# Gated-output copies kept in their traced order, and a new slot order in the recurrence, of a two-layer hybrid trunk

## The chip, the cores and the metric

The kernel runs on one core of one Trainium2 chip. The metric is the device time of one execution in microseconds (us); lower is better. The core's engines run side by side, each through its own queue in order: TensorE (PE) does the matrix products, VectorE (DVE), ScalarE (ACT) and GpSimd (POOL) the element-wise work, and SyncE (SP) starts the transfers (DMA).

## The reference

One sequence of 1024 positions and 1024 features in float32 goes through two layers and a last norm. Each layer is `x = x + gate(c) * mixer(rmsnorm(x) * (1 + scale(c)) + shift(c))`, where shift, scale and gate are products of `silu(c)` with a matrix. Layer 0 is attention: eight heads of windowed attention (A) and eight of forgetting attention (B, softmax with a decay), whose outputs are gated and go through one output projection:

```
y = jnp.concatenate([a_out, b_out], axis=-1) * jax.nn.silu(gate)
return y @ w_out
```

Layer 1 is a gated linear recurrence over positions. Its input product has 8 blocks of 128 features for the recurrence (`xr`) and 8 for the gate:

```
xc = conv_b
for j in range(CONV_WIDTH):
    xc = xc + xp[:, j:j + S] * conv_w[j]
r = sigmoid(xc_block @ w_a + b_a);  i = sigmoid(xc_block @ w_x + b_x)
log_a = -LRU_C * r * softplus(-lam);  a = exp(log_a)
u = sqrt(-expm1(2.0 * log_a)) * (i * xc)
hs[t] = a[t] * hs[t - 1] + u[t]
y = (hs * silu(gate)) @ w_out
```

## The kernel before

**Products.** Every float32 operand is written as a sum of a high and a low part in the format that PE multiplies at full rate. Of a weight, ACT copies the high part (`whi_...`) and POOL subtracts it from the raw one, which leaves the low part (`wlo_...`). Each block of 128 x 128 weights then takes three matmuls: high x high, low x high, high x low. Activations are split in the same way (`yh`/`yl`, `y1h`/`y1l`, `xch`/`xcl`, `pth`/`ptl`). A "copy" below is ACT's making of a high part, a "subtraction" that of a low one.

**Layer 0.** The attention heads are written out as a list of small steps, and `weave` mixes into them the matmuls of the next projection (`fill`), so that PE has work while softmax goes on. In the stretch that matters here (the seventh call of `weave`, 420 to 460 us) PE runs the last B heads: scores `sB`, transposes of the probabilities `ptB`, which `split_t` splits into `pth_B` and `ptl_B`, and the product with the values, `oB`. Mixed in are the last weights of K and V (`khb`, `klb`, `vb`) and the output projection of the first half of the positions (`ps_fill<-yh,...`, weights `whi_o0a`, `wlo_o0a`). That projection needs the gated outputs `gy` of finished heads in split form: `split_act` copies `yh` on ACT and subtracts `yl` on POOL. Six such splits are put in a list `drip`, and `fill` takes one off it every eighth matmul. Their place on an engine is not the place in the code: here a scheduler orders the instructions of ACT, by its own simulated times, except those that are issued under `paced("act")`.

**Layer 1.** From `ordered |= ALL` on, every engine keeps the order of the code. `slot(c)` does feature block c: sigmoids `r`, `i` and `th` on ACT, `a`, `a2`, the square root, `hs` by a scan on DVE; meanwhile PE makes the input products of block c+2 (`ps_lx`, with the convolution's taps on DVE into `xc`) and the gate product of block c (`ps_lg`, in two halves h of 512 positions). The gated output of one half is made in three steps: `gate_s` (sigmoid `sg` on ACT, a multiplication by `ps_lg` on DVE), `gate_a` (times `hs`, on POOL), `gate_b` (copy `y1h` on ACT, subtraction `y1l` on POOL). `split_next` splits the next 128 columns of weights in two halves (`whi_lg` twice on ACT, `wlo_lg` twice on POOL, or `lx`); `split_r` splits the small weights of r and i (`wrh`, `wrl`). `mod_late` is a dot product of the late rows of the modulation on DVE. `last_slot(7)` has no `ps_lx`; it splits the first weights of the output product, `whi_wo`/`wlo_wo` by `split_next` and the later ones by `split_out(e)`. Then the output product of the first half of the positions (`ps_o`) runs over e = 0 to 7 with k over the 8 feature blocks. For e below `AHEAD` its last feature block, k = 7, is put off until the first seven blocks of all these e are through.

In the text, t0(c) is the start of DVE's multiplication `sg_r<-ps_lg,sg_r` of half 0 in slot c; the loop's period is the distance from one to the next.

Of the kernel before, what the change touches and what calls it, by code (L numbers as in the profile page):

```python
# [3 lines left out]

# [1 line left out]

# [13 lines left out]
EARLY = 12  # L20
NS = 5
FIRST = 18
AHEAD = 3
RUN = 32
P = 128
S = 1024
# [22 lines left out]
def hybrid_trunk(  # L49
# [53 lines left out]
    def copy(out, in_, scale=1.0):  # L103
        act.activation(out, in_, AF.Copy, scale=scale)
# [612 lines left out]
    def scores(ps, q, n, kh, kl, ks):  # L717
# [2 lines left out]
        mm(ps, q[:, nq], kh[:, ks], start=True, stop=False)  # L720
        mm(ps, q[:, nq], kl[:, ks], start=False, stop=True)

    def split_t(pt, w, name):
        hi = at.tile([P, HALF], F32R, tag="pth", name=f"pth_{name}")
        lo = at.tile([P, HALF], F32R, tag="ptl", name=f"ptl_{name}")
        copy(hi[:, :w], pt[:, :w])
        sub(dve, lo[:, :w], pt[:, :w], r32(hi[:, :w]))
        return hi, lo

# [217 lines left out]
    def fill(jobs, ahead=lambda: None):  # L947

        jobs = list(jobs)
        ws = {0: jobs[0][0]()}  # L950
        for n, (_, ks, xs, use) in enumerate(jobs):
            if n + 1 < len(jobs):
                ws[n + 1] = jobs[n + 1][0]()
            else:
                ahead()
            w = ws.pop(n)
            for h, (xhi, xlo) in xs().items():
                ps = ps_mm(f"ps_fill_{h}")
                cnt = 0
                for k in ks:  # L960
                    whi, wlo = w[k]
                    for i, (a, b) in enumerate(((whi, xhi), (wlo, xhi), (whi, xlo))):
                        mm(ps, a, b[:, k], start=(k == ks[0] and i == 0), stop=(k == ks[-1] and i == 2))
                        cnt += 1
                        if late and cnt == 9:
                            late.pop()()
                        if drip and cnt % 8 == 0:
                            drip.popleft()()
                        yield MM
                x = use(h, ps)  # L970
                if x:
                    late.append(x)
# [120 lines left out]
    def total(js):  # L1093
        return sum(len(ks) * 3 * len(list(xs())) * MM for _, ks, xs, _ in js)
# [262 lines left out]

    def mod_late(c):
        mod_row(late_rows.pop(c), 24 + c)
        load_row(c + 2)  # L1360

    def rt(tag, c, dt=F32, w=S, bufs=1):
        return rp.tile([P, w], dt, tag=tag, name=f"{tag}_r{c}", bufs=bufs)
# [66 lines left out]
    def gate_a(c, h, eng=gp):  # L1430

        mul(eng, sgs[c, h], sgs[c, h], hss[c][:, half(h)])
# [9 lines left out]
        load_next()  # L1442
    load_r(0)
    load_row(0)
    load_row(1)
    for c in range(2):
        conv(c, 0, ps01[c])()
    split_xc(0, half(0))
# [15 lines left out]
    def slot(c):  # L1464
        n = c + 2
        w = ready.popleft()
        if c == 0:
            ps_x = proj1(0, f"lx_{n}", 0, w)
        ps = gates(c)
        if c == 0:  # L1470
            split_next()
        else:
            gate_s(c - 1, 1)
            gate_a(c - 1, 1)
        r, i_ = sig_ri(c, ps)

        th, a_, a2 = rt("th", c), rt("a", c), rt("a2", c)
        act.activation(th, r, AF.Tanh, scale=sp[:, c : c + 1])
        mul(dve, i_, i_, xcs[c])
        split_xc(c + 1)  # L1480
        split_r(c + 1)
        if n < KT:
            load_r(n)
        if c:
            gate_b(c - 1, 1)
        act.activation(a_, r, AF.Exp, scale=nsp[:, c : c + 1])
        if c:
            split_next()
        if n < KT:
            taps = conv(n, 0, proj1(0, f"lx_{n}", 0, w) if c else ps_x)  # L1490
        act.activation(a2, a_, AF.Square)
        if n < KT:
            taps()
        dve.scalar_tensor_tensor(out=th, in0=a2, scalar=1.0, in1=th, op0=ALU.add, op1=ALU.mult)
        act.activation(th, th, AF.Sqrt, bias=tiny)
        mul(dve, i_, i_, th)
        hs_ = hss[c] = rt("hs", c, bufs=2)
        dve.tensor_tensor_scan(out=hs_, data0=a_, data1=i_, initial=0.0, op0=ALU.mult, op1=ALU.add)
        if n < KT:
            conv(n, 1, proj1(0, f"lx_{n}", 1, w))()  # L1500
            w = ready.popleft()
            split_next()
        lgs[c, 0] = proj1(0, f"lg_{c}", 0, w)
        gate_s(c, 0)
        gate_a(c, 0)
        if n < KT:
            gate_b(c, 0)
        mod_late(c)
        lgs[c, 1] = proj1(0, f"lg_{c}", 1, w)

    def last_slot(c):

        w = ready.popleft()
        ps = gates(c)
        for h in range(2):
            lgs[c, h] = proj1(0, f"lg_{c}", h, w)
        r, i_ = sig_ri(c, ps)
        split_next()
        wout.append(ready.popleft())
        gate_s(c - 1, 1)  # L1520
        gate_b(c - 1, 0)
        th, a_, a2 = rt("th", c), rt("a", c), rt("a2", c)
        act.activation(th, r, AF.Tanh, scale=sp[:, c : c + 1])
        mul(dve, i_, i_, xcs[c])
        gate_s(c, 0)
        gate_a(c - 1, 1)
        act.activation(a_, r, AF.Exp, scale=nsp[:, c : c + 1])
        mod_late(c)
        act.activation(a2, a_, AF.Square)
        gate_b(c - 1, 1)  # L1530
        dve.scalar_tensor_tensor(out=th, in0=a2, scalar=1.0, in1=th, op0=ALU.add, op1=ALU.mult)
        split_out(1, dve)
        act.activation(th, th, AF.Sqrt, bias=tiny)
        mul(dve, i_, i_, th)
        hs_ = hss[c] = rt("hs", c, bufs=2)
        dve.tensor_tensor_scan(out=hs_, data0=a_, data1=i_, initial=0.0, op0=ALU.mult, op1=ALU.add)
        split_out(2)
        gate_a(c, 0, dve)
        gate_s(c, 1)
        gate_b(c, 0, dve)  # L1540
        gate_a(c, 1, dve)
        split_out(3)
        gate_b(c, 1, dve)

    for c in range(KT - 1):
# [6 lines left out]
    for t0, tw in ((0, 512), (512, 256), (768, 256)):  # L1552
# [7 lines left out]
        for e in range(KT):  # L1560
            if t0 == 0 and e + 4 < KT:
                split_out(e + 4)
            w = wout[e]
            nm = f"ps_o1_{t0}_{e}"
            ps = (ps_s, ps_t)[e % 2](nm) if t0 == 0 and e <= AHEAD else ps_1(nm)
            last = KT - 1 if t0 == 0 and e < AHEAD else KT
            gemm(ps[:, :tw], w, y1h[:, :, ts], y1l[:, :, ts], range(last), last=(last == KT))
            late_.append((e, w, ps))
            if t0 == 0 and e + 1 < AHEAD:
                continue  # L1570
            for e_, w_, ps in late_:
# [94 lines left out]
```

## Time and profile before

| | |
|---|---|
| median of 3 runs | 886.59 us (886.31 to 886.68) |
| the profiled execution | 888.44 us |
| its span, first to last instruction | 886.7 us |
| PE busy | 860.7 us, 97% of the span |
| DVE, ACT, POOL busy | 564.5, 535.7, 378.1 us (64%, 60%, 43%) |
| mean granted clock of PE | 0.986 |

Of PE's time 3% is waiting, but a matmul at the lower clock also counts as busy. So two things are read together: the idle time that stands in square brackets behind an instruction, with the engine and tile that ended it, and the granted clock of a stretch (PEclk; 1.00 is 2.4 GHz, 0.50 is 1.2 GHz). All instructions of this kernel carry line L85, so they are told apart by the names of their tiles; out stands left of the arrow, in right of it.

### The profile page before, as it was taken

Reading aid. Unit: us, or ns where it says so; the run is one execution under the profiler, and the core shown is the slowest. Engines: PE = TensorE matmul, PEld = TensorE weight load, DVE = VectorE, ACT = ScalarE, POOL = GpSimd, SP = SyncE. Lnnn points to the kernel's source line nnn. Section 1 sums busy time; section 2 is a strip of 40 time slices with the busy share of each in tenths; the row PEclk is TensorE's granted clock in tenths of the full one; section 3 lists DMA queues with packets and bytes.
Section 4 is the critical chain, followed back from the end, with each engine's and each line's share of the span. In section 5 each row is a group of like instructions: output and inputs, shape, how many; then the busy total and the mean of one; then the engine's idle time right before and its main releaser. Section 6 shows DMA issues by size and latency. Waiting matters only on the chain.

```text
span 886.7 us, 13483 instructions
## 1 busy us (share of the span) xinstructions
PE 860.7 (97%) x4618; PEld 730.7 (82%) x4618; DVE 564.5 (64%) x1136; ACT 535.7 (60%) x1047; POOL 378.1 (43%) x427
## 2 busy tenths in 40 slices
PE   9999999999989999999999999999899999999995
PEld 8887898888878888888777888878688877878995
DVE  7886657688676565565656668276556666583453
ACT  5765124788676666566656647358666667774432
POOL 4843322343342232331744656532565555475100
PEclk9999999999999999999999999999899999999998
DMA  9944772100013322322373564421212212126042
GB/s 344 404 185 127 216 229 60 49 25 20 30 53 111 107 80 101 123 87 78 110 240 104 184 209 145 145 79 44 78 54 72 77 57 67 56 71 226 7 149 83
DMA packets 54620, 103.83 MB, mean 117 GB/s; under 512 B 6960, under 2 KB 20720, under 8 KB 54040
## 3 DMA queue, kind: packets, MB, share of 16 engines
q1 hardware_dynamic: 53400, 101.93, 34.8%
q10 hardware_dynamic: 1152, 1.05, 0.5%
q8 instruction: 36, 0.59, 0.3%
q14 instruction: 32, 0.26, 0.1%
HBM read 94.02 MB, written 8.93 MB: 116 GB/s over the span
## 4 chain that ended last, share of the span: by engine, by line
PE 66%; ACT 11%; DVE 10%; DMA 5%; POOL 4%; issue 3%; SPq 0%; DVEq 0%; POOLq 0%; ACTq 0%
PE ps_fill L85 22%; PE ps_o L85 10%; PE pst L85 5%; PE ps_o0c L85 5%; PE oB L85 4%; PE sB L85 4%; PE ptB L85 3%; DVE xc_r L85 3%; PE ps_v L85 3%; DVE hs_r L85 2%; DMA ada<-in_ada_dram 2%; PE ps_lx L85 2%; POOL sg_r L85 2%; PE sA L85 2%; PE ps_lg L85 2%
## 5 line engine op out<-in xcount | busy, mean ns | idle before, releaser
L85 PE MATMUL ps_o<-y1h,wo 128*128 128x256 f32 (+1 forms) x336 | 76.8, 323 | 2.2 <-DVE wo L85 1.1
L85 DVE TENSOR_TENSOR ptl_B<-ptB,pth_B 128x512 fp32r<-128x512 f32 (+1 forms) x80 | 50.8, 636 | 36.8 <-ACT pth_B L85 36.3
L85 ACT ACTIVATE pth_B<-ptB 128x512 fp32r<-128x512 f32 (+1 forms) x80 | 44.0, 551 | 44.6 <-PE ptB L85 43.7
L85 ACT ACTIVATE pB<-pB,mnB 128x128 f32<-128x128 f32 (+3 forms) x64 | 49.5, 774 | 31.3 <-DVE mnB L85 25.9
L85 PEld LDWEIGHTS ps_o<-y1h,wo 128*128 128x128 f32 x336 | 56.7, 192 | 7.5 <-ACT wo L85 1.5
L85 POOL TENSOR_SCALAR_AFFINE_SELECT pB<-pB 128x128 f32<-128x128 f32 x64 | 18.8, 296 | 96.3 <-DMA pB<-gd 71.6
L85 PE MATMUL pst<-hh,ws 128*128 128x512 f32 x192 | 55.3, 396 | 0.1
L85 PE MATMUL ps_o<-y1l,wo 128*128 128x256 f32 (+1 forms) x168 | 54.2, 323 | 0.0
L85 PE MATMUL ps_lg<-h1h,wlo_lg 128*128 128x512 f32 x128 | 51.3, 401 | 2.3 <-POOL wlo_lg L85 2.3
L85 PE MATMUL ps_lg<-h1h,whi_lg 128*128 128x512 f32 x128 | 51.4, 401 | 1.9 <-ACT whi_lg L85 1.9
L85 DVE SCALAR_TENSOR_TENSOR xc_r<-ps_lx,col,xc_r 128x509 f32<-128x509 f32 (+2 forms) x48 | 35.7, 745 | 24.6 <-ACT xt_r L85 23.5
L85 PE MATMUL ps_lg<-h1l,whi_lg 128*128 128x512 f32 x128 | 50.8, 397 | 0.0
L85 PE MATMUL ps_lx<-h1l,whi_lx 128*128 128x512 f32 x128 | 50.3, 393 | 0.2 <-POOL h1l L85 0.2
L85 PE MATMUL ps_lx<-h1h,whi_lx 128*128 128x512 f32 x128 | 50.3, 393 | 0.0
L85 PE MATMUL ps_lx<-h1h,wlo_lx 128*128 128x512 f32 x128 | 50.1, 391 | 0.0
L85 DVE CUSTOM_DVE_ANT_0 pB<-sB,pB 128x384 f32<-128x384 f32 (+2 forms) x64 | 35.4, 554 | 19.4 <-PE sB L85 9.3
L85 ACT ACT_TABLE_LOAD x35 | 44.9, 1283 | 3.6 <-issue 1.9
L85 PE MATMUL ptB<-ident,pB 128*128 128x128 f32 x288 | 45.1, 273 | 1.2 <-DVE ptl_B L85 0.7
L85 PEld LDWEIGHTS ptB<-ident,pB 128*128 128x128 f32 x288 | 35.8, 140 | 12.2 <-PE rbT_B L85 1.5
L85 POOL TENSOR_TENSOR wlo_lx<-raw_lx,whi_lx 128x512 fp32r<-128x512 f32 x16 | 30.6, 1929 | 32.0 <-ACT whi_lx L85 30.1
L85 PEld LDWEIGHTS pst<-hh,ws 128*128 128x128 f32 x192 | 35.9, 188 | 9.0 <-DVE mod L85 0.6
L85 ACT ACTIVATE sq_o<-x 128x512 f32<-128x512 f32 (+1 forms) x33 | 18.0, 545 | 33.3 <-DVE x L85 33.1
(313 smaller groups left out, 2838.7 us busy)
## 6 DMA issues: line engine op xcount, KB each, us to landing
ada<-in_ada_dram SPq DMA_DIRECT2D x32, 512.0 KB
x<-in_xT_dram SPq DMA_DIRECT2D x20, 256.0 KB
ada<-in_ada_dram SPq DMA_DIRECT2D x4, 1024.0 KB
pB<-gd SPq DMA_DIRECT2D x8, 512.0 KB
raw_o0a<-in_wo_dram SPq DMA_DIRECT2D x16, 256.0 KB
raw_o0c<-in_wo_dram SPq DMA_DIRECT2D x16, 256.0 KB
x1d<-x SPq DMA_DIRECT2D x16, 256.0 KB
raw_lx<-in_wl_dram SPq DMA_DIRECT2D x16, 256.0 KB
```

The costliest lines, as they stand in the source:

```text
L85: ins = issue(*args, **kw)
```

## The change

1. A list `dripping` is filled during the last call of `weave`. While it is, the copies `pth` of `split_t` are issued under `paced("act")`, and so are the splits that `fill` takes off `drip`: these two kinds of copies keep their order of the code among each other on ACT.
2. In `slot(c)` the splits of the small weights and of the next gate weights come right behind the sigmoids r and i, and the gated output of slot c-1 is finished later: `gate_a` of half 1 and `gate_b` of both halves stand behind `split_xc` of slot c. Before, `gate_b` of half 0 was the end of slot c itself.
3. The late rows of the modulation are loaded one slot ahead, not two.
4. In `last_slot` the split of `wo_1` goes from DVE to POOL, `split_out(2)` and `(3)` come one step earlier, and the gated output of block 6 is finished later.
5. `AHEAD` is 4, not 3: k = 7 of e = 0, 1, 2 (9 matmuls) comes behind the k < 7 of e = 3 (21 matmuls).

The core of the diff:

```
     def split_t(pt, w, name):
...
-        copy(hi[:, :w], pt[:, :w])
+        with paced("act") if dripping else nullcontext():
+            copy(hi[:, :w], pt[:, :w])
...
                         if drip and cnt % 8 == 0:
-                            drip.popleft()()
+                            with paced("act"):
+                                drip.popleft()()
...
     for i in range(7):
+        dripping[:] = [1] * (i == 6)
         weave(slots[cuts[i] : cuts[i + 1]], fill(...), ...)
...
         ps = gates(c)
-        if c == 0:
-            split_next()
-        else:
+        if c:
             gate_s(c - 1, 1)
-            gate_a(c - 1, 1)
         r, i_ = sig_ri(c, ps)
+        split_r(c + 1)
+        if n < KT:
+            load_r(n)
+        split_next()
 
         th, a_, a2 = rt("th", c), rt("a", c), rt("a2", c)
         act.activation(th, r, AF.Tanh, scale=sp[:, c : c + 1])
         mul(dve, i_, i_, xcs[c])
         split_xc(c + 1)
-        split_r(c + 1)
-        if n < KT:
-            load_r(n)
         if c:
+            gate_a(c - 1, 1)
+            gate_b(c - 1, 0)
             gate_b(c - 1, 1)
         act.activation(a_, r, AF.Exp, scale=nsp[:, c : c + 1])
-        if c:
-            split_next()
...
         gate_a(c, 0)
-        if n < KT:
-            gate_b(c, 0)
         mod_late(c)
+        load_row(c + 1)
...
     def last_slot(c):
...
-        gate_a(c - 1, 1)
+        split_out(1)
...
-        gate_b(c - 1, 1)
...
-        split_out(1, dve)
+        split_out(2)
...
-        split_out(2)
+        gate_a(c - 1, 1)
+        split_out(3)
         gate_a(c, 0, dve)
         gate_s(c, 1)
         gate_b(c, 0, dve)
         gate_a(c, 1, dve)
-        split_out(3)
+        gate_b(c - 1, 1)
```

In layer 0, ACT's queue around the first splits of `gy` (in the last call of `weave`, near 420 us of the profile) read before:

```order
L85 ACTIVATE pth_B_3_2_4835<-ptB_3_2_4830 128x512
L85 ACTIVATE yh_4895<-gy_511 128x512 x4
L85 ACTIVATE khb_0_4855<-ps_fill_4728 64x512
L85 ACTIVATE yh_4895<-gy_511 128x512 x2
L85 ACTIVATE pth_B_3_3_4851<-ptB_3_3_4847 128x384
L85 ACTIVATE pth_B_0_0_4880<-ptB_0_0_4876 128x384
L85 ACTIVATE khb_0_4855<-ps_fill_4728 64x512
L85 ACTIVATE khb_1_4856<-ps_fill_4728 64x512
L85 ACTIVATE tmp<-oB_3_4823 64x256
```

and now:

```order
L85 ACTIVATE pth_B_3_2_4835<-ptB_3_2_4830 128x512
L85 ACTIVATE khb_0_4855<-ps_fill_4728 64x512
L85 ACTIVATE pth_B_3_3_4851<-ptB_3_3_4847 128x384
L85 ACTIVATE khb_0_4855<-ps_fill_4728 64x512
L85 ACTIVATE khb_1_4856<-ps_fill_4728 64x512
L85 ACTIVATE pth_B_0_0_4880<-ptB_0_0_4876 128x384
L85 ACTIVATE tmp<-oB_3_4823 64x256
L85 ACTIVATE yh_4895<-gy_511 128x512
L85 ACTIVATE tmp<-oB_0_4913 64x256
```

The six copies `yh` stood ahead of `pth_B_3_3` and `pth_B_0_0`; now none does, and the six come one by one behind later steps. Further on, `pth_B_1_1` now stands behind three `khb` copies and the two `whi_o0a` copies, where it stood ahead of them, and on DVE `ptl_B_3_1` of the following head stands ahead of the `pB_0` and `pB_1` that wait for a transfer.

In slot 1, ACT's queue from the second half of r on (c = 1; slots 2 to 5 have the same pattern) read before:

```order
L85 ACTIVATE r_r_7017<-psr_1_6998,col 128x512
L85 ACTIVATE i_r_7018<-psi_0_7005,col 128x512
L85 ACTIVATE i_r_7018<-psi_1_7006,col 128x512
L85 ACTIVATE th_r_7023<-r_r_7017,sp 128x1024
L85 ACTIVATE xch_r_7028<-xc_r_6881 128x1024
L85 ACTIVATE wrh_r_6874<-wr_r_6872 128x128
L85 ACTIVATE wrh_r_6878<-wr_r_6876 128x128
L85 ACTIVATE y1h<-sg_r_1_7013 128x512
L85 ACT_TABLE_LOAD
L85 ACTIVATE a_r_7024<-r_r_7017,nsp 128x1024
L85 ACTIVATE whi_lg_0_7047<-raw_lg_0_6851 128x512
L85 ACTIVATE whi_lg_1_7053<-raw_lg_1_6930 128x512
```

and now:

```order
L85 ACTIVATE r_r_7012<-psr_1_6994,col 128x512
L85 ACTIVATE i_r_7013<-psi_0_7001,col 128x512
L85 ACTIVATE i_r_7013<-psi_1_7002,col 128x512
L85 ACTIVATE wrh_r_6851<-wr_r_6849 128x128
L85 ACTIVATE wrh_r_6855<-wr_r_6853 128x128
L85 ACTIVATE whi_lg_0_7030<-raw_lg_0_6867 128x512
L85 ACTIVATE whi_lg_1_7036<-raw_lg_1_6928 128x512
L85 ACTIVATE th_r_7042<-r_r_7012,sp 128x1024
L85 ACTIVATE xch_r_7047<-xc_r_6879 128x1024
L85 ACTIVATE y1h<-sg_r_0_6961 128x512
L85 ACTIVATE y1h<-sg_r_1_7009 128x512
L85 ACT_TABLE_LOAD
```

The two `whi_lg` copies moved from behind `a` to ahead of `th`, and the two `y1h` copies stand together ahead of the table load.

On POOL, the same slot from the first gated half on read before (`sg_r_0`, `sg_r_1` are the halves' products with `hs`):

```order
L85 TENSOR_TENSOR sg_r_0_6963<-sg_r_0_6963,hs_r_6892 128x512
L85 TENSOR_TENSOR y1l<-sg_r_0_6963,y1h 128x512
L85 TENSOR_TENSOR sg_r_1_7013<-sg_r_1_7013,hs_r_6892 128x512
L85 TENSOR_TENSOR wrl_r_6875<-wr_r_6872,wrh_r_6874 128x128
L85 TENSOR_TENSOR wrl_r_6879<-wr_r_6876,wrh_r_6878 128x128
L85 TENSOR_TENSOR y1l<-sg_r_1_7013,y1h 128x512
L85 TENSOR_TENSOR wlo_lg_0_7048<-raw_lg_0_6851,whi_lg_0_7047 128x512
L85 TENSOR_TENSOR wlo_lg_1_7054<-raw_lg_1_6930,whi_lg_1_7053 128x512
L85 TENSOR_TENSOR wlo_lx_0_7130<-raw_lx_0_6936,whi_lx_0_7129 128x512
L85 TENSOR_TENSOR wlo_lx_1_7136<-raw_lx_1_7051,whi_lx_1_7135 128x512
```

and now:

```order
L85 TENSOR_TENSOR sg_r_0_6961<-sg_r_0_6961,hs_r_6890 128x512
L85 TENSOR_TENSOR wrl_r_6852<-wr_r_6849,wrh_r_6851 128x128
L85 TENSOR_TENSOR wrl_r_6856<-wr_r_6853,wrh_r_6855 128x128
L85 TENSOR_TENSOR wlo_lg_0_7031<-raw_lg_0_6867,whi_lg_0_7030 128x512
L85 TENSOR_TENSOR wlo_lg_1_7037<-raw_lg_1_6928,whi_lg_1_7036 128x512
L85 TENSOR_TENSOR sg_r_1_7009<-sg_r_1_7009,hs_r_6890 128x512
L85 TENSOR_TENSOR y1l<-sg_r_0_6961,y1h 128x512
L85 TENSOR_TENSOR y1l<-sg_r_1_7009,y1h 128x512
L85 TENSOR_TENSOR wlo_lx_0_7128<-raw_lx_0_6934,whi_lx_0_7127 128x512
L85 TENSOR_TENSOR wlo_lx_1_7134<-raw_lx_1_7034,whi_lx_1_7133 128x512
```

Both `y1l` and the product of half 1 moved behind the four weight splits; the two `wlo_lg` moved ahead of them.

## Rows read from the trace of the kernel before

**Rows 1.** The page, part 1: busy, share of the span, instructions.

```profile
PE 860.7 (97%) x4618; PEld 730.7 (82%) x4618; DVE 564.5 (64%) x1136; ACT 535.7 (60%) x1047; POOL 378.1 (43%) x427
```

**Rows 2.** One slot each: length, busy by engine, PEclk, DMA share, GB/s.

```profile
621.36:651.81 30.45, 27.97 (x109) 22.17 (x108) 20.37 (x27) 17.50 (x25) 16.91 (x12) 0.89 0.23 69
651.81:676.38 24.57, 24.57 (x109) 20.27 (x108) 14.47 (x18) 17.51 (x25) 14.37 (x10) 1.00 0.22 66
...
726.76:752.61 25.85, 25.00 (x109) 20.19 (x108) 15.75 (x19) 17.50 (x25) 14.89 (x10) 1.00 0.21 67
...
780.00:806.00 26.00, 23.82 (x97) 19.02 (x96) 18.03 (x16) 14.71 (x19) 17.23 (x11) 0.93 0.44 138
```

**Rows 3.** The same columns for three stretches behind a wait of PE.

```profile
424.13:429.00 4.87, 4.72 (x17) 4.09 (x18) 4.09 (x8) 2.48 (x6) 4.73 (x7) 0.65 0.39 118
...
637.00:644.20 7.20, 6.50 (x15) 4.81 (x16) 4.58 (x5) 5.92 (x10) 2.51 (x2) 0.53 0.25 74
...
786.00:791.00 5.00, 3.90 (x9) 2.87 (x10) 4.08 (x4) 3.42 (x4) 2.46 (x2) 0.66 0.31 103
```

**Rows 4.** PE, 424 to 456 us: start, took, instruction, [idle before].

```profile
424.13 0.44 PE L85 MATMUL oB<-pth_B,vb 128*128 128x256 f32 x2 [1.43 <-ACT pth_B L85]
...
450.10 0.41 PE L85 MATMUL rbT_B<-ident,rb_B 128*128 128x128 f32 x2 [0.86 <-DVE ptl_B L85]
...
455.09 0.50 PE L85 MATMUL oB<-ptl_B,vb 128*128 128x256 f32 x2 [1.15 <-DVE ptl_B L85]
```

**Rows 5.** ACT, order of time, 418 to 426 us.

```profile
422.56 1.13 ACT L85 ACTIVATE yh<-gy 128x512 fp32r<-128x512 f32 x2
423.61 0.84 ACT L85 ACTIVATE pth_B<-ptB 128x384 fp32r<-128x384 f32 x2
```

**Rows 6.** PE, order of time, 635 to 640 and 785 to 791 us.

```profile
637.11 0.75 PE L85 MATMUL ps_lg<-h1h,whi_lg 128*128 128x512 f32 x1 [1.89 <-ACT whi_lg L85]
638.45 0.80 PE L85 MATMUL ps_lg<-h1h,wlo_lg 128*128 128x512 f32 x1 [0.59 <-POOL wlo_lg L85]
...
786.00 0.49 PE L85 MATMUL ps_o<-y1h,wo 128*128 128x512 f32 x1 [1.08 <-ACT wo L85]
787.59 0.79 PE L85 MATMUL ps_o<-y1h,wo 128*128 128x512 f32 x1 [1.10 <-DVE wo L85]
```

**Rows 7.** DVE, order of time, 676 to 703 us (slot 3).

```profile
676.35 0.68 DVE L85 TENSOR_TENSOR sg_r<-ps_lg,sg_r 128x512 f32<-128x512 f32 x1
...
682.88 1.23 DVE L85 TENSOR_TENSOR i_r<-i_r,xc_r 128x1024 f32<-128x1024 f32 x1 [1.55 <-ACT i_r L85]
...
702.20 0.68 DVE L85 TENSOR_TENSOR sg_r<-ps_lg,sg_r 128x512 f32<-128x512 f32 x1
```

**Rows 8.** POOL, order of time, the same stretch.

```profile
677.12 2.27 POOL L85 TENSOR_TENSOR sg_r<-sg_r,hs_r 128x512 f32<-128x512 f32 x1 [2.52 <-DVE sg_r L85]
...
681.41 1.30 POOL L85 TENSOR_TENSOR sg_r<-sg_r,hs_r 128x512 f32<-128x512 f32 x1
685.11 1.72 POOL L85 TENSOR_TENSOR wrl_r<-wr_r,wrh_r 128x128 fp32r<-128x128 f32 x2 [2.40 <-ACT wrh_r L85]
...
688.81 2.55 POOL L85 TENSOR_TENSOR wlo_lg<-raw_lg,whi_lg 128x512 fp32r<-128x512 f32 x2 [0.71 <-ACT whi_lg L85]
695.91 4.52 POOL L85 TENSOR_TENSOR wlo_lx<-raw_lx,whi_lx 128x512 fp32r<-128x512 f32 x2 [4.55 <-ACT whi_lx L85]
```

**Rows 9.** ACT, order of time, the same stretch.

```profile
685.10 0.65 ACT L85 ACTIVATE y1h<-sg_r 128x512 fp32r<-128x512 f32 x1
...
688.12 1.13 ACT L85 ACTIVATE whi_lg<-raw_lg 128x512 fp32r<-128x512 f32 x2
```

**Rows 10.** ACT, order of time, 771 to 800 us.

```profile
774.93 1.27 ACT L85 ACTIVATE i_r<-psi,col 128x512 f32<-128x512 f32 x2 [0.67 <-DVE hs_r L85]
776.09 1.15 ACT L85 ACTIVATE whi_wo<-raw_wo 128x512 fp32r<-128x512 f32 x2
```

**Rows 11.** POOL, order of time, 771 to 800 us.

```profile
777.72 3.54 POOL L85 TENSOR_TENSOR wlo_wo<-raw_wo,whi_wo 128x512 fp32r<-128x512 f32 x2
```

More of the change, by code (lines that the diff above doesn't have):

```diff
@@ L2 @@
 import math
-from contextlib import ExitStack, contextmanager
+from contextlib import ExitStack, contextmanager, nullcontext
 import numpy as np
@@ L22 @@
 FIRST = 18
-AHEAD = 3
+AHEAD = 4
 RUN = 32
@@ L721, in scores @@
         mm(ps, q[:, nq], kl[:, ks], start=False, stop=True)
+    dripping = []
     def split_t(pt, w, name):
@@ L1174, in hybrid_trunk @@
     for i in range(7):
+        dripping[:] = [1] * (i == 6)
         weave(slots[cuts[i] : cuts[i + 1]], fill(jobs[i + 1], jobs[i + 2][0][0]), total(jobs[i + 1]), 0 if i else FIRST)
+    dripping.clear()
     def square_sum(sqa, xn, e, pool, name, tag="sq"):
@@ L1359, in mod_late @@
         mod_row(late_rows.pop(c), 24 + c)
-        load_row(c + 2)
     def rt(tag, c, dt=F32, w=S, bufs=1):
@@ L1444, in hybrid_trunk @@
     load_row(0)
-    load_row(1)
     for c in range(2):
@@ L1564, in hybrid_trunk @@
             nm = f"ps_o1_{t0}_{e}"
-            ps = (ps_s, ps_t)[e % 2](nm) if t0 == 0 and e <= AHEAD else ps_1(nm)
+            ps = (ps_s, ps_t)[e % 2](nm) if t0 == 0 and e < AHEAD else ps_1(nm)
             last = KT - 1 if t0 == 0 and e < AHEAD else KT
```

## The prediction

> **What bounds the kernel.** I first read the busy shares: PE is busy 97% of the span and no other engine above 64% [rows 1]. A change of ordering can therefore only win what PE waits, and what it loses when its clock falls behind a wait. Next I cut the recurrence into slots. A slot in which PE never waits takes 24.57 us at clock 1.00; slot 1 takes 30.45 at clock 0.89, slots 4 and 5 some 25.85 each, and the slot in which the output product begins 26.00 at clock 0.93 [rows 2]. PE's own record names the waits: in slot 1 1.89 us for `whi_lg` and 0.59 for `wlo_lg`, at the output product 1.08 and 1.10 us for the split of `wo_1` [rows 6], in layer 0 1.43 us for `pth_B`, 0.86 and 1.15 for `ptl_B` [rows 4]. Behind the larger ones the clock falls: 0.53 of full over 7.20 us, 0.66 over 5.00, 0.65 over 4.87 [rows 3], a loss of (1 - clock) x length = 3.38, 1.70 and 1.70 us. Slot 1 shows that such sums hold: 1.89 + 0.59 + 3.38 = 5.86, and its slot is 30.45 - 24.57 = 5.88 longer than a free one.
>
> The sums below are made against the profiled execution, 888.44 us; it lies 1.85 above the median of the runs shown.
>
> **Part 1, the copies in layer 0.** At 424.13 PE waits for two `pth_B` copies, which start at 423.61 because ACT makes two `yh` first (422.56, 1.13 us) [rows 4, 5], and four more ahead of those. With all six behind, the copies are ready before PE comes: 1.43 + 1.70 = 3.1 us gained. The six copies and their subtractions cost nothing where they now stand: the projection that reads `yh` is mixed in only after the next head's steps, and POOL idles between. But at about 434 `pth_B_1_1` now has three `khb` and two `whi_o0a` copies ahead of it. One copy of 512 columns is 0.57 us (1.13 for two) [rows 5], and 434 had two of these five to spare, so I estimate 0.95 us of waiting there. At 450.10 the wait for the head's `ptl_B` and the transpose behind it was 0.86 [rows 4]; two more copies on ACT ahead of it make about 0.8 more. The 1.15 us at 455.09 [rows 4] goes, since `ptl_B` no longer stands behind work that waits for a transfer. Sum: -3.1 + 0.95 + 0.8 - 1.15 = -2.5. The 450 wait is then about 1.7 us, longer than the 1.43 behind which the clock fell [rows 3, 4]; I take one more such loss of 1.70 there. Ends of that price: 0 (at 450.10 and 455.09 nothing fell) and 3.38 (slot 1). **Part 1: -0.8.** The Trainium skill, "TensorE: Matmul & The Clock Gate", Part 1, says that the gate's window runs free, so that what a given wait does depends on where it falls; by that either end may come, and the trace, where waits of 1.08 + 1.10 lost 1.70 and a wait of 0.86 nothing, does not speak against it.
>
> **Part 2, slot 1.** `whi_lg` no longer waits on ACT for half 0 of the gated output, nor for th, `xch`, the table and `a`. In the new order ACT reaches it straight behind i, and POOL the low part behind one product and two small ones. I get the first `wlo_lg` at t0(0) + 6.97 (below). t0(0) itself is later by some 0.9, since slot 0 now makes these two copies ahead of th (1.13 us [rows 9]). Two periods of 25.85 before 676.35 [rows 7] it was at 624.7; that gives 625.6, and 632.6 for `wlo_lg`. PE wants `whi_lg` at 637.11 - 1.89 = 635.2 [rows 6]. So the waits and the low clock of slot 1 go: **-5.9**.
>
> **Part 3, the loop of slots 2 to 6.** From t0 = 676.35 to 702.20 the loop's period is 25.85 [rows 7], so the loop of ACT, DVE and POOL is the bound there, not PE's 24.57; slots 2 and 3 are free only because slot 1 left PE behind, and slots 4 and 5 pay 1.28 each [rows 2]. What sets the new period is when POOL reaches half 1, because `y1h` of half 1 now stands ahead of the table and `a`. POOL and DVE hinder each other: the same product of POOL takes 2.27 us beside the dot product of DVE and 1.30 alone, and a pair of `wlo_lx` 4.52 beside the scan where a pair of `wlo_lg` takes 2.55 [rows 8]. So I add their operations up in turn from t0: product of half 0 done at +2.87 (a little before the +3.04 of 677.12 + 2.27, the dot product being the same), i x xc and `xcl` some 1.22 each [rows 7], one small `wrl` some 0.41 uncovered: +5.72. Two `wlo_lg` of 1.25: first at +6.97, second at +8.22. Product of half 1, 1.29: +9.51. Then `y1h` of half 1 begins at +9.57. Before, it began at 685.10 - 676.35 = +8.75, and 17.10 us later came the next t0 [rows 7, 9]; of these the two `whi_lg`, 1.04 without their overlap, are gone. Period: 9.57 + 17.10 - 1.04 = 25.63. Bounds: PE's 24.57 from below; from above one of the POOL operations that moved takes 3.28 instead of 1.29, as the second `wlo_lx` does (4.52 less a free 1.24 for the first) [rows 8], which gives 27.6. I take 25.63, since the row that POOL and DVE now share is that of short operations in turn.
>
> At 25.63 `wlo_lg` falls 1.06 per slot behind PE's 24.57. The slack is 635.2 - 632.6 = 2.6 us in slot 1, then 1.5, 0.5, and gone in slot 4: PE waits 0.6 in slot 4, 1.06 in slot 5, about 0.4 in the shorter slot 6. So PE is ahead of its old self by 5.88 + 2 x 1.28 - 2.06 = 6.3 at the end of slot 7's gate products, while the loop is nowhere: 625.6 + 5 x 25.63 = 753.7, against 702.20 + 2 x 25.85 = 753.9 before.
>
> **Part 4, the last slot.** Hence PE comes to the output product at 780.0 - 6.3 = 773.7 and finds no weights. `whi_wo` ended at 776.09 + 1.15 = 777.24 [rows 10]. It gains 0.2 with the loop, 0.67 because the sigmoids i no longer wait [rows 10], and about 1.0 from `whi_lg` made earlier: 775.3. `wlo_wo` began at 777.72 and took 3.54 for two [rows 11]; its first half I put at 777.6. So PE waits 1.6 and 2.1, and the clock falls for about 2.0 (between the 1.70 of this place and the 3.38 of slot 1 [rows 3]): 5.7. In return `wo_1` is split on POOL ahead of the exponential's table, and e = 1's waits with their clock go: 1.08 + 1.10 + 1.70 = 3.9, or 26.00 less 96 matmuls of 24.57/108 = 0.2275, 4.2 [rows 2]. Net of this part: 5.7 - 4.2 = +1.5, and together with the 6.3: -4.8. `AHEAD` = 4 puts k = 7 of three products 21 x 0.2275 = 4.8 us later. What it needs, block 7's gated output, follows the loop, which does not move; PE comes 4.8 earlier by the sum and 4.8 later by this, so it costs and gains nothing, with about 1 us of cover by my count. Transfers of the modulation's rows start a slot later and still land a slot before use. Later splits of `wo` push the square sums back, which I put at +0.3. **Parts 2 to 4: -4.5.**
>
> Sum: -0.8 - 4.5 = -5.3; 888.44 - 5.3 = 883.1 profiled, **881.2** as a median.
>
> **Rivals.** (a) *The loop keeps up with PE* (20%). POOL and DVE need not exclude each other in the new row: i x xc read beside `wrl` unharmed would bring +9.51 down by up to 2.4. Then every slot takes PE's 24.57, the loop is 5 x 1.06 = 5.3 earlier and the weights are there when PE comes: 5.88 + 2.56 in the slots and 4.2 behind them, -12.6; with part 1 between -0.8 and -2.5 that is 871.5 to 873.2. The 2.27 against 1.30 speaks against it [rows 8]. The Trainium skill, "SBUF — State Buffer", section "SBUF: two separate sides", states a lock on a shared port pair, held for a whole instruction, between GpSimd and a VectorE operation with two SBUF inputs; the rows agree, and by it the period is the 25.63.
>
> (b) *The gain is eaten* (13%). PE waits at the output product and at 450 as long as it was ahead, with a full 3.38 us of low clock at both: -5.3 + 1.4 + 1.7 + 1 for the last k = 7 steps, which lose their cover: about -1, 887 to 885.
>
> (c) *Slower: POOL's new row lengthens the loop* (11%). `gate_a` of half 1 stands behind four weight splits, and `a` behind it. From a period of 26.7 on, five slots x 1.1 more use up the 5.3. At the upper bound of 27.6 the loop is 10 us later at the last slot, and everything behind waits for it: -5.3 + 10 = +4.7, 891. The 3.28 speaks for it; against it that the scan, DVE's only long operation, is not beside this row.
>
> (d) *The copies do not move the wait* (in (b)'s chance): PE waits at 434 and 450 for as long as at 424; part 1 is 0.
>
> The forecast, -2 to -8, has the rest, 56%. A change within 0.2%, 1.8 us, can hardly be told from none by a measurement of this kernel. Faster: 56 + 20 and a little of (b) make 0.77; the same 0.12; slower 0.11. The range of 8 in 10 runs from the middle of (a), 872, to the end of (b), 888; the forecast's own is 878 to 885.
>
> **What would show it.** Right: no wait of `oB` at 424 and full clock there; no wait of `ps_lg` in slot 1; t0 to t0 near 25.6 with small waits of `ps_lg` for `wlo_lg` in slots 4 to 6; one wait of `ps_o` for `whi_wo` and `wlo_wo` at its first matmuls, none for `wo_1`. Wrong: a period of 24.6 or of over 26.5, a fall of the clock that is missing or that comes elsewhere, or a wait of e = 4 or of k = 7 for `y1l`.

## The result and the profile after

The changed kernel takes 882.49 us (median of 5 runs, 882.07 to 883.34), the kernel before 886.68 in the same session (5 runs): a ratio of 0.9947, with a 95% interval of 0.9934 to 0.9961. The forecast was 881.2, in a range of 872 to 888. The profiled execution took 882.07 us, with a span of 880.3; against the profiled one of before it is 6.4 shorter; the medians differ by 4.2. The forecast change of 5.3 lies between the two, and the experiments below bear on where their difference comes from.

PE's record in layer 0 (start, took, instruction, idle before), which answers to [rows 4]:

```profile
434.65 0.45 PE L85 MATMUL oB<-pth_B,vb 128*128 128x256 f32 x2 [0.52 <-ACT pth_B L85]
435.27 0.45 PE L85 MATMUL oB<-ptl_B,vb 128*128 128x256 f32 x2 [0.17 <-DVE ptl_B L85]
...
448.56 0.41 PE L85 MATMUL rbT_B<-ident,rb_B 128*128 128x128 f32 x2 [1.76 <-DVE ptl_B L85]
```

and two stretches of it by windows (the column behind POOL's is PEclk), the first of which answers to the first of [rows 3]:

```profile
422.45:425.20 2.75, 2.75 (x18) 2.48 (x17) 2.44 (x5) 1.69 (x5) 1.29 (x4) 1.00 0.72 253
...
448.50:453.00 4.50, 4.44 (x30) 3.96 (x31) 2.47 (x8) 2.18 (x6) 2.06 (x4) 1.00 0.71 218
```

The wait of 1.43 us at 424 is gone and the clock is full where it was 0.65. The wait at 434 that the forecast expected is there (0.52 + 0.17), and the one near 450 has grown from 0.86 to 1.76; when the transposes for `pth_B` come (445.50), ACT is still at two `whi_o0a` copies (445.26, 1.13 us), which before were over by then (446.50 against 447.94). In this execution no clock fell behind that wait. The one of 1.15 at 455 is gone.

The slots by windows, which answer to [rows 2] and, in the last line, to the third of [rows 3]:

```profile
621.30:645.87 24.57, 24.57 (x110) 20.27 (x109) 15.26 (x17) 16.97 (x25) 15.01 (x10) 1.00 0.22 70
...
695.01:719.80 24.79, 24.39 (x106) 19.51 (x105) 15.38 (x19) 16.75 (x26) 14.99 (x10) 1.00 0.22 69
719.80:745.30 25.50, 24.99 (x109) 19.97 (x109) 16.10 (x19) 17.47 (x25) 15.71 (x11) 1.00 0.21 68
773.00:780.20 7.20, 5.43 (x13) 4.06 (x14) 4.48 (x5) 5.70 (x9) 7.20 (x5) 0.55 0.22 73
```

Slot 1 is as long as a slot without a wait, 24.57 us, where it was 30.45. Slots 4 and 5 are 0.22 and 0.93 us longer than that (0.6 and 1.06 were worked out). Behind 773 the clock is 0.55 of full. The start of DVE's multiplication of half 0 in slots 1, 2 and 5, by DVE's record as in [rows 7]:

```profile
648.51 0.68 DVE L85 TENSOR_TENSOR sg_r<-ps_lg,sg_r 128x512 f32<-128x512 f32 x1
...
674.18 0.68 DVE L85 TENSOR_TENSOR sg_r<-ps_lg,sg_r 128x512 f32<-128x512 f32 x1
...
751.14 0.68 DVE L85 TENSOR_TENSOR sg_r<-ps_lg,sg_r 128x512 f32<-128x512 f32 x1
```

Four periods take 751.14 - 648.51 = 102.63 us, 25.66 each; 25.63 was worked out. In slot 3 POOL does, as in [rows 8]:

```profile
674.94 2.27 POOL L85 TENSOR_TENSOR sg_r<-sg_r,hs_r 128x512 f32<-128x512 f32 x1 [2.53 <-DVE sg_r L85]
677.18 2.84 POOL L85 TENSOR_TENSOR wrl_r<-wr_r,wrh_r 128x128 fp32r<-128x128 f32 x2
679.98 2.53 POOL L85 TENSOR_TENSOR wlo_lg<-raw_lg,whi_lg 128x512 fp32r<-128x512 f32 x2
682.48 1.28 POOL L85 TENSOR_TENSOR sg_r<-sg_r,hs_r 128x512 f32<-128x512 f32 x1
```

The first product still takes 2.27 us beside the dot product. The two small subtractions `wrl` now take 2.84 for both, where they took 1.72: DVE's `i x xc` (676.59, 1.71 us) and `xcl` (678.22, 1.48) are both beside them now, where before only `xcl` was (684.87, 1.22). The first `wlo_lg` begins at t0 + 5.80 (+5.72 was worked out), half 1 at +8.30 (+8.22). ACT in the same stretch, as in [rows 9], waits for it:

```profile
683.79 0.63 ACT L85 ACTIVATE y1h<-sg_r 128x512 fp32r<-128x512 f32 x1 [5.90 <-POOL sg_r L85]
```

`y1h` of half 1 begins at t0 + 9.61 (+9.57 was worked out) behind 5.90 us of idling, and the next t0, 699.85, comes 16.06 later, which is the 17.10 less 1.04 of the forecast. The later loads of the modulation's rows cost nothing that shows: no dot product of DVE waits for one. The start of the output product, as in [rows 6, 10, 11], by PE, ACT and POOL:

```profile
773.00 0.49 PE L85 MATMUL ps_o<-y1h,whi_wo 128*128 128x512 f32 x1 [1.65 <-ACT whi_wo L85]
775.26 0.79 PE L85 MATMUL ps_o<-y1h,wlo_wo 128*128 128x512 f32 x1 [1.77 <-POOL wlo_wo L85]
```

```profile
772.32 1.15 ACT L85 ACTIVATE whi_wo<-raw_wo 128x512 fp32r<-128x512 f32 x2
```

```profile
773.94 3.50 POOL L85 TENSOR_TENSOR wlo_wo<-raw_wo,whi_wo 128x512 fp32r<-128x512 f32 x2
```

PE is there early and waits 1.65 us for `whi_wo` and 1.77 for `wlo_wo` (1.6 and 2.1 were forecast), and starts at half clock. The waits for `wo_1` are gone.

The same matmul in both traces (in the last row but one, the last matmul of e = 0 to 3, whose order differs) tells what each place brought:

| place | starts before / after, us | ahead by | step, measured | step, forecast |
|---|---|---|---|---|
| behind 424 | 428.68 / 425.19 | 3.5 | -3.5 | -3.1 |
| behind 434 | 437.77 / 435.27 | 2.5 | +1.0 | +0.95 |
| `rbT_B` near 450 | 450.10 / 448.56 | 1.5 | +1.0 | +0.8, and +1.7 of clock |
| `oB` at 455 | 455.09 / 452.25 | 2.8 | -1.3 | -1.15 |
| slot 1, from 637 on | 644.10 / 635.35 | 8.75 | -5.9 | -5.9 |
| before the output product's waits (773.00 - 1.65) | 780.00 / 771.35 | 8.65 | +0.1 | -0.5 |
| 13th matmul of e = 0 of the output product | 782.72 / 780.12 | 2.6 | +6.1 | +5.7 |
| last of the 96 matmuls of e = 0 to 3 | 805.78 / 799.18 | 6.6 | -4.0 | -4.2 |
| end of the span | 886.7 / 880.3 | 6.4 | +0.2 | +0.3 |

### The profile page after: what moved, and what is told of

Same layout as the page of the kernel before. It is cut to its first block, busy times and chain, and to the rows that moved or that the text cites. A ratio compares the mean times of both kernels' runs of the same rounds, so it can differ in the third digit from the quotient of the medians.

```text
span 880.3 us, 13493 instructions
## 1 busy us (share of the span) xinstructions
PE 857.9 (97%) x4618; PEld 728.0 (83%) x4618; DVE 561.5 (64%) x1134; ACT 536.9 (61%) x1047; POOL 385.6 (44%) x429
## 4 chain that ended last, share of the span: by engine, by line
PE 77%; issue 6%; POOL 5%; DMA 4%; DVE 3%; ACT 3%; SPq 0%; POOLq 0%; DVEq 0%; ACTq 0%
PE ps_fill L85 23%; PE ps_o L85 10%; PE ps_lx L85 6%; PE pst L85 6%; PE ps_o0c L85 5%; PE ps_lg L85 5%; PE oB L85 4%; PE sB L85 4%; PE ptB L85 4%; PE ps_v L85 3%; DMA ada<-in_ada_dram 2%; PE sA L85 2%; PE oA L85 1%; POOL wlo_lg L85 1%; PE ptA L85 1%
## 5 line engine op out<-in xcount | busy, mean ns | idle before, releaser
L85 ACT ACTIVATE y1h<-sg_r 128x512 fp32r<-128x512 f32 x16 | 10.0, 632 | 44.9 <-POOL sg_r L85 39.8
```

Of the source, the lines that this page charges most:

```text
L85: ins = issue(*args, **kw)
```

## Experiments

Each ratio is to the kernel before in the same session, whose median lay between 886.61 and 887.44 us; differences from the changed kernel are between medians of different sessions.

The reading to be tested was this. ACT, DVE and POOL form a loop over the slots that sets when the output product finds its weights. In POOL's queue the product of half 1 with `hs` stands behind four weight splits and delays `y1h`, the table and `a`. Slot 1's gain is only lead for PE, which it waits away in front of that loop.

### One part at a time

`drip_only`: the kernel before with the edits of `split_t`, `fill` and `dripping` alone (the first three pieces of the diff above).

> The kernel before with the layer-0 part alone (paced pth and yh copies). Theory (each step moves PE's own waits by what the traces show, and the recurrence starts as much earlier): the wait for pth_B at 424 and its low clock go, waits near 434 and 449 take part of it back, net -2.8 us at 455, and all behind keeps its shape, slot 1 and the start of the output product with their waits: 883.8 us (ratio 0.9968). Rival (the rows at 449 are near the point at which the clock falls): the clock falls behind the 1.8 us wait in most executions, net -1.1: 885.5 (0.9987).

Measured: 884.28 us (12 runs), 0.9978 [0.9968, 0.9989]: -2.3, between the two but nearer to the first.

`slots_only`: the kernel before with `slot` and the loads of the rows as changed, and nothing else.

> The kernel before with the recurrence's new slot order and the later loads of the rows alone; the last slot, AHEAD and layer 0 as before. Theory (the loop of ACT, DVE and POOL sets when the output product's first weights and wo_1 are there, PE's gain in slot 1 is only lead): period 25.6 against 25.85, PE reaches the output product some 6 us earlier, waits there for whi_wo and wlo_wo, and again for wo_1 near 785.5 and 787 as before: 0 to -0.8 us, 886.2 (0.9995). Rival (slot 1's 5.9 us is kept behind the slots): -4 or more, 882.5 (0.995).

Measured: 884.62 us (12 runs), 0.9984 [0.9971, 0.9997]: -2.0. Most of slot 1's 5.9 us is indeed lost again, but more is left than expected: PE waits 1.6 + 1.8 us at the output product's first weights, and the two waits for `wo_1` are still there, with 0.43 and 1.09.

`last_only`: the kernel before with `last_slot` as changed and `AHEAD = 4`.

> The kernel before with the last slot's new order and AHEAD = 4 alone; slots 0 to 6 and layer 0 as before. Theory (the waits for wo_1 were the ones that set the end, slot 1's were only in front of a slower loop): slot 1 keeps its 5.9 us, PE reaches the output product at 780 as before without a wait, the waits for wo_1 and their low clock go: -4.0 us, 882.6 (0.9955), as much as all of the recurrence's parts gave together. Rival (the parts need each other): wo_1 on POOL comes behind y1l and the waits move to e = 1 or 2 or to k = 7: -1 or less, 885.6 (0.999).

Measured: 884.98 us (12 runs), 0.9985 [0.9972, 0.9998]: -1.6, less than half of what was expected. The waits for `wo_1` are gone and slot 1 keeps its own. But 1.7 of the 4.0 was low clock, which not every execution has (below), and at e = 4 PE waits 0.61 us for a later split of `wo` and further on 0.67 for the sum of squares `sqa`, which it doesn't in the changed kernel. POOL begins that split at 799.47 and PE comes to e = 4 at 799.82; in the changed kernel the two are 797.60 and 799.41. So the split is 1.9 us later here and PE only 0.4. Why the split is later by that much was not followed up.

`old_slots`: the changed kernel with `slot` and the loads of the rows as before the change.

> The changed kernel with slots 0 to 6 as before the change: layer 0, the last slot and AHEAD = 4 are new. Theory (slot 1's gain is only lead, which is waited away at the output product's first weights because the loop comes no earlier): as fast as the changed kernel within 1 us, 882.0 to 883.5, with slot 1's waits, no wait at the output product's first weights. Rival (the new slots carry the gain): 884.5, the layer-0 part alone.

Measured: 882.72 us (6 runs), 0.9954 [0.994, 0.9967], the changed kernel's 882.49 within its spread. So in this combination the new slot order, the largest part of the diff, brings nothing that can be measured. PE's record of slot 1 there, and its window:

```profile
633.73 0.49 PE L85 MATMUL ps_lg<-h1h,whi_lg 128*128 128x512 f32 x1 [1.87 <-ACT whi_lg L85]
635.07 0.50 PE L85 MATMUL ps_lg<-h1h,wlo_lg 128*128 128x512 f32 x1 [0.85 <-POOL wlo_lg L85]
```

```profile
633.90:641.00 7.10, 6.25 (x27) 4.90 (x28) 4.72 (x6) 5.82 (x9) 2.53 (x3) 1.00 0.23 75
```

The waits of slot 1 are back, 1.87 + 0.85 us, and in each of slots 2 to 5 PE waits 0.84 or 0.85 more for `wlo_lg`; they are paid, and those at the output product's first weights aren't there.

### What sets the loop

`half1_first` moves one line of the changed kernel back:

```
             gate_s(c - 1, 1)
+            gate_a(c - 1, 1)
         r, i_ = sig_ri(c, ps)
...
         if c:
-            gate_a(c - 1, 1)
             gate_b(c - 1, 0)
             gate_b(c - 1, 1)
```

> The changed kernel with gate_a(c - 1, 1), the product of half 1 with hs, ahead of the splits of the small weights and of lg in POOL's row, where it was before the change. Theory (POOL's row ahead of that product sets y1h, the exponential and with it the period): y1h of half 1 begins near t0 + 5.5 instead of + 9.6, the loop has 3 us to spare, every slot takes PE's 24.57, no ps_lg waits in slots 4 to 6 (1.5 us), the loop arrives 5.4 earlier at the last slot and most of the 1.65 + 1.77 us of waits of the output product with the 3.2 us of low clock go: -7 us against the changed kernel, 875.5. Rival (the period is set by ACT's own row or by DVE's): period stays at 25.5 or more, 882 to 883.

Measured: 872.49 us (4 runs), 0.9841 [0.9823, 0.9859]: 10 us below the changed kernel, more than expected. DVE's multiplication of half 0, POOL and ACT behind the first of them, and PE at the output product:

```profile
644.85 0.68 DVE L85 TENSOR_TENSOR sg_r<-ps_lg,sg_r 128x512 f32<-128x512 f32 x1
...
666.83 0.68 DVE L85 TENSOR_TENSOR sg_r<-ps_lg,sg_r 128x512 f32<-128x512 f32 x1
```

```profile
645.61 4.52 POOL L85 TENSOR_TENSOR sg_r<-sg_r,hs_r 128x512 f32<-128x512 f32 x2 [2.53 <-DVE sg_r L85]
650.08 1.87 POOL L85 TENSOR_TENSOR wrl_r<-wr_r,wrh_r 128x128 fp32r<-128x128 f32 x2
651.92 2.54 POOL L85 TENSOR_TENSOR wlo_lg<-raw_lg,whi_lg 128x512 fp32r<-128x512 f32 x2
```

```profile
650.09 1.14 ACT L85 ACTIVATE y1h<-sg_r 128x512 fp32r<-128x512 f32 x2
651.24 1.28 ACT L85 ACT_TABLE_LOAD   x1
```

```profile
768.78 0.39 PE L85 MATMUL ps_o<-y1h,whi_wo 128*128 128x512 f32 x1
769.01 0.39 PE L85 MATMUL ps_o<-y1h,wlo_wo 128*128 128x512 f32 x1
```

The period is 21.98 us while the loop catches up (PE's 24.57 sets it later on); `y1h` follows at t0 + 5.24 (two copies), not + 9.61. The output product's first two matmuls come 0.23 apart, without a wait, at full clock. PE is there 2.6 us earlier than in the changed kernel (768.78 against 773.00 - 1.65), where 1.5 was expected, and the waits there are gone with all of their low clock, where most of it was expected to go.

`dot_early` leaves that line where the change put it and moves another one:

```
         act.activation(th, th, AF.Sqrt, bias=tiny)
+        mod_late(c)
+        load_row(c + 1)
         mul(dve, i_, i_, th)
...
         gate_a(c, 0)
-        mod_late(c)
-        load_row(c + 1)
```

> The changed kernel with mod_late(c), DVE's dot product, moved from behind gate_a(c, 0) to ahead of the multiplication i x th, where DVE waits 1.2 us for ACT's square root and POOL idles. Theory (POOL and DVE exclude each other for whole operations, so the dot product of 1.27 us holds up everything that POOL does behind t0): POOL's first product takes 1.3 instead of 2.27 us, all behind it up to y1h of half 1 comes about 1.0 earlier, period 24.6 to 24.7 instead of 25.66, the waits of ps_lg in slots 4 to 6 go, those of the output product's first weights shrink to under 0.5 and its clock stays up: -7 us against the changed kernel, 875.5. Rival (the dot product runs beside POOL, the product's 2.27 has another cause): period 25.6 as now, 882.5.

Measured: 875.4 us (4 runs), 0.9871 [0.9853, 0.989]. POOL's record, and two starts of DVE's multiplication (both halves in one row here):

```profile
672.84 1.30 POOL L85 TENSOR_TENSOR sg_r<-sg_r,hs_r 128x512 f32<-128x512 f32 x1 [2.53 <-DVE sg_r L85]
674.09 2.85 POOL L85 TENSOR_TENSOR wrl_r<-wr_r,wrh_r 128x128 fp32r<-128x128 f32 x2
676.90 2.53 POOL L85 TENSOR_TENSOR wlo_lg<-raw_lg,whi_lg 128x512 fp32r<-128x512 f32 x2
```

```profile
672.08 1.28 DVE L85 TENSOR_TENSOR sg_r<-ps_lg,sg_r 128x512 f32<-128x512 f32 x2
...
696.76 1.28 DVE L85 TENSOR_TENSOR sg_r<-ps_lg,sg_r 128x512 f32<-128x512 f32 x2
```

The same product of POOL takes 1.30 instead of 2.27 us, the row behind it is a us earlier, and the period is 24.68. Nothing on POOL was changed: the dot product on DVE had held it up. The rival is out. PE waits for nothing at the output product's first weights; waits of 0.35 and 0.66 us for later splits of `wo` and of 0.30 for `sqa` are left, which `half1_first` does not have. The Trainium skill, "SBUF — State Buffer", section "SBUF: two separate sides", has a VectorE operation with two SBUF inputs and a GpSimd operation hold the shared port pair in turn; the 2.27 against 1.30 and the `wrl` pair's 2.84 against 1.72 agree with it.

`slots_half1` asks whether that line's place alone decides over the slots: the kernel before with the new slot order, but `gate_a(c - 1, 1)` ahead of `sig_ri`; all else as before.

> The kernel before with the new slot order alone, but gate_a(c - 1, 1) kept where it was (ahead of the splits); last slot, AHEAD = 3 and layer 0 as before the change. It differs from the run of the new slots alone in one line's place. Theory (POOL's row ahead of that product is all that keeps the slots' gain from the end): slots at PE's 24.57, no wait at the output product's first weights nor for wo_1, but with AHEAD = 3 PE comes to k = 7 some 2.5 us before block 7's gated output: 886.7 - 14.1 + 2.3 (layer 0) + 2.5 = 877.4, 874.9 if k = 7 does not wait. Rival (the gain of half 1 first needs the last slot's new order or layer 0): 882 to 884, like the new slots alone.

Measured: 876.47 us (6 runs), 0.9865 [0.984, 0.989], against 884.62 for the same kernel with that line further down. k = 7 does not wait, so with the loop in time `AHEAD` = 3 is enough. The runs lie apart (873.6 to 877.4); in the profiled one, of 877.39, the wait at 455 of layer 0, which ends with a transfer (POOL's `pB` waits 5.23 us for it), is longer than the 1.15 of [rows 4], and the clock behind the wait at 424 is 0.65 again:

```profile
456.57 0.50 PE L85 MATMUL oB<-ptl_B,vb 128*128 128x256 f32 x2 [2.77 <-DVE ptl_B L85]
```

### The rest of the last slot, and the two kinds of paced copies

`ahead3`: the changed kernel with one number as before, and the bank that goes with it:

```
-AHEAD = 4
+AHEAD = 3
...
-            ps = (ps_s, ps_t)[e % 2](nm) if t0 == 0 and e < AHEAD else ps_1(nm)
+            ps = (ps_s, ps_t)[e % 2](nm) if t0 == 0 and e <= AHEAD else ps_1(nm)
```

> The changed kernel with AHEAD = 3. Theory (AHEAD = 4 gives block 7's gated output the time that PE's earlier arrival takes away): PE comes to k = 7 some 4.8 us earlier, near 791.9 of the changed kernel's trace, where y1l of block 7 was ready at 794.6; it waits 2.7 us there for y1h or y1l, and the clock may fall behind it by up to 3.2: 885 to 888. Rival (block 7's output was there anyway): 882.5.

Measured: 884.62 us (12 runs), 0.9972 [0.9961, 0.9984], 2.1 above the changed kernel. PE's record and two windows:

```profile
793.01 0.50 PE L85 MATMUL ps_o<-y1h,whi_wo 128*128 128x512 f32 x1 [2.61 <-ACT y1h L85]
```

```profile
773.00:781.00 8.00, 6.59 (x22) 5.25 (x23) 4.47 (x5) 6.50 (x9) 8.00 (x6) 0.79 0.19 66
788.00:803.00 15.00, 12.39 (x54) 9.64 (x53) 9.30 (x8) 5.46 (x10) 9.03 (x7) 1.00 0.68 229
```

The wait is 2.61 us, as worked out (2.7), but the clock stays full behind it. So `AHEAD = 4` is what keeps the gain from being waited away at k = 7 while the loop is late.

`half1_old_last`: the kernel with half 1 first, with `last_slot` as before the change.

> The kernel with the product of half 1 ahead of the splits, with the last slot's order as before the change (AHEAD stays 4). Theory (with the loop no longer in the way, the late split of wo_1 is a wait of its own): PE waits for wo_1's two parts at e = 1 as before the change, 1.1 + 1.1 us or more, with 1.7 to 3.2 us of low clock: +4, 876.5. Rival (the earlier loop takes this wait away too): 872.5.

Measured: 872.27 us (5 runs), 0.9838 [0.9822, 0.9855]. The theory missed here and the rival holds: with the loop no longer late, ACT copies `wo_1` at

```profile
769.13 1.14 ACT L85 ACTIVATE wo<-raw_wo 128x512 fp32r<-128x512 f32 x2
```

and DVE its low part by 769.78 + 2.18 = 771.96; PE, which began e = 0 at 768.23, wants it 21 matmuls later, at 772.99. In these runs the last slot's new order is worth something only while the loop is late.

`yh_only`: the changed kernel with the `pth` copies left to the scheduler:

```
-        with paced("act") if dripping else nullcontext():
-            copy(hi[:, :w], pt[:, :w])
+        copy(hi[:, :w], pt[:, :w])
```

> The changed kernel with only the yh copies paced, the pth copies left to the scheduler. On ACT pth_B_1_1 then stands ahead of the two whi_o0a copies again; the yh copies stay behind the two pth of 424. Theory (each wait is work that stands ahead of it on ACT): 424 stays without a wait, the wait of 0.52 and 0.17 us near 434 goes, the one of 1.76 near 449 stays: -0.8, 881.7. Rival (it is the order of pth that took the 424 wait away): the wait at 424 is back with 1.4 us and its low clock, +2 or more, 884.5.

Measured: 880.78 us (6 runs), 0.9935 [0.9921, 0.995]. The wait at 424 stays away, so it is the place of the `yh` copies that took it away, and the one at 434 is gone. The one near 450 stays (1.87 us, now ended by POOL's `wlo_o0a`), and behind it the clock of this execution is 0.66 over 4.50 us.

`yh_half1` is both edits, `yh_half1_dot` has the dot product moved as well.

> Both: only the yh copies paced, and the product of half 1 ahead of the splits in the slots. Theory: the two places are far apart and have nothing between them that waits for a transfer, so the gains add: 0.8 below the kernel with half 1 first, 871.7. Rival (what layer 0 gains is waited away later): as that kernel, 872.5.

> Only the yh copies paced, the product of half 1 ahead of the splits, and the dot product ahead of i x th. Theory (with half 1 first the loop already has over 2 us to spare in every slot, PE's 24.57 sets the pace): nothing more to gain there, 871.7 as without the last edit. Rival (POOL's row is still late somewhere behind the slots, at wlo_wo or in the last slot): 870.5 or less.

Measured: 871.67 us (4 runs), 0.983 [0.9815, 0.9845], and 871.6 us (4 runs), 0.9831 [0.9813, 0.9848]. The first has the fewer edits and is 10.8 us below the changed kernel; the second adds nothing that can be measured, as both remedies end the same wait.

### What a low clock costs

Two of these kernels repeat a wait of the kernel before, untouched by their edits. `slots_only` has layer 0's wait at 424:

```profile
423.93 0.45 PE L85 MATMUL oB<-pth_B,vb 128*128 128x256 f32 x2 [1.43 <-ACT pth_B L85]
```

```profile
424.00:428.90 4.90, 4.75 (x26) 4.02 (x27) 4.23 (x8) 2.58 (x6) 4.75 (x7) 1.00 0.36 109
...
776.00:784.00 8.00, 6.72 (x21) 5.01 (x21) 6.64 (x7) 6.71 (x9) 7.26 (x5) 0.79 0.21 66
```

The wait is the same 1.43 us as in [rows 4], yet the clock behind it is 1.00, not 0.65. In `slots_half1`, which differs from `slots_only` only in one line of the slots, far behind this place, the wait is 1.43 again and the clock is 0.65:

```profile
424.00:428.90 4.90, 4.75 (x17) 4.04 (x18) 3.88 (x7) 2.17 (x5) 4.76 (x7) 0.65 0.30 101
```

In `old_slots` the waits of slot 1 were 1.87 + 0.85 us and the clock 1.00 (its window above), where before 1.89 + 0.59 were followed by 0.53 [rows 3, 6]. So the fall belongs to one execution, not to the wait alone. Over all traces that hold a wait, the granted clock in a stretch that begins where it ends (in slot 1 and at the output product it holds the second wait too) is:

| the wait | stretch, us | granted clock, trace by trace |
|---|---|---|
| 1.43 us at 424 | 4.87 | 0.65 (before), 1.00 (`slots_only`), 1.00 (`last_only`), 0.65 (`slots_half1`) |
| 1.87 or 1.89 us in slot 1 | 7.20 | 0.53 (before), 0.76 (`drip_only`), 0.76 (`last_only`), 1.00 (`old_slots`) |
| 1.64 or 1.65 us at the output product | 7.20 | 0.55 (changed), 0.76 (`slots_only`), 0.76 (`ahead3`), 0.56 (`yh_only`) |
| 1.76 to 1.87 us near 450 | 4.50 | 0.66 (`yh_only`), 1.00 in the nine others |

The times go the same way. In 68 runs of the kernel before, from 884.55 to 890.41 us, the 13 with a mean granted clock of 0.987 or less have a median of 888.1, the 14 with 0.994 or more one of 885.2. The four runs of `half1_first`, which has few waits left, lie between 871.71 and 872.85. The Trainium skill, "TensorE: Matmul & The Clock Gate", Part 1, has the gate's window run free, not from the kernel's start. The traces above, with different clocks behind the same wait, agree with that, if what a wait does depends on where in the window it falls; no run here shows the window itself.

## Why the prediction was right, and where it was off

The direction and the size hold, and the chain of causes is the one that was forecast. Its steps by the table: slot 1's 5.9 us, the period 25.63 against 25.66, the waits at the output product, the new waits at 434 and 450, all within 0.6 us. That the loop is what binds, and that its length comes from POOL's row taken in turn with DVE, is shown by `half1_first` and `dot_early`, which end it in two ways.

Part 1, the copies: the sum of the waits was -2.5 and measured -2.8; the 1.7 us of clock added to it did not come in the profiled execution (PEclk 1.00 behind 1.76 us of waiting). The forecast had named a fall of the clock that is missing as a sign of being wrong, and in this term it was: it took as certain a loss that one of ten traces with this wait shows (`yh_only`, 0.34 x 4.50 = 1.5). Part 4: the low clock at the output product was put at 2.0. By the window it is 0.45 x 7.20 = 3.2, but 1.77 us of that window is waiting, in which a low clock loses nothing. By PE's record the 13th matmul of e = 0 starts 780.12 - 773.00 = 7.12 us behind the first, where before it was 782.72 - 780.00 = 2.72; less the wait of 1.77 the low clock cost 2.6. The two pieces of low clock were thus mis-sized both ways, by -1.7 and +0.6. With the -0.4 at 424, the +0.6 in slots 4 to 6 and the smaller terms of the table the profile shows -6.4 where -5.3 was forecast. That the errors of the clock partly cancel is luck.

The term that made the median come out 1.3 above the forecast is the step "it lies 1.85 above the median of the runs shown", which was carried over whole to the changed kernel. That distance goes with low clock: the profiled execution of before fell at 424, in slot 1 and at the output product, all at 0.53 to 0.66 [rows 3], its mean clock of 0.986 is at the low end of the 68 runs, and `slots_only`, `old_slots` and `last_only` show the same or like waits with less or none. The change takes away the waits, and with them a loss that the median execution had probably paid only in part. So the profiled change of 6.4 is larger than the median's 4.2: of the 2.2 between them 1.76 is the distance of the profiled execution of before from the median of 886.68, and 0.42 that of the changed kernel's, which lies below its own. How often an execution has each fall was not measured beyond the traces above.

What the prediction costed at nothing: `AHEAD = 4` was said to neither cost nor gain. With it no wait came, as said; without it the wait of 2.61 us shows what it covers.

Of the rivals, (a), the loop that keeps up with PE, was given 871.5 to 873.2; `half1_first`, in which it does, though by another order and not because POOL and DVE run freely side by side, took 872.49. What spoke against it, the 2.27 us beside 1.30, was rightly read. Rival (b) names a part of what happened, waits and low clock at the output product that take back most of slot 1's gain. For (c), the period did not lengthen: 25.66 against 25.85.

Within the whole change the new slot order turned out worthless (`old_slots`), and alone it brought 2.0 (`slots_only`): it took PE's wait out of slot 1 and put it in front of the output product. One line in it, the product of half 1 put behind the splits, cost the 10 us that the rest would have brought.

## What to carry to other kernels

A wait that is removed from the busy engine is only lead until the loop of the other engines is shorter too: work out the loop's period and compare it with the busy engine's own pace before a gain is counted to the end. When a queue's order is changed, look at what the moved operation releases: here the last product of a half released a table load and an exponential, and had to stand ahead of splits that nobody was waiting for yet. Where a clock falls behind waits, price the waits from a trace, but the low clock as something that one execution has and the next has not, and don't carry a profile's distance from the median over to the changed kernel.

## What was not expected of the hardware

The same wait of 1.43 us was followed by a granted clock of 0.65 in one execution and of 1.00 in another, and a single wait of 2.61 us by 1.00. A small subtraction on POOL (128 x 128) takes 0.46 us at the median of the kernel before and 1.44 at that of the changed one, where DVE operations of two inputs run beside both of a pair (1.72 to 2.84 us for the two); a product of 128 x 512 takes 1.30 without such a neighbour and 2.27 beside the dot product, while DVE's own `i x xc` went from 1.23 [rows 7] to 1.71 in the changed kernel: each side pays for the other.
